# Scoring the paged keys of a decode step on TensorE, with one softmax over all eight requests

## The chip, the core and the metric

The kernel runs on one core of a Trainium2 chip. The metric is the device time of one execution in microseconds, from runs on the chip. Engines are named as in the profile: PE (matrix multiplies; PEld is its weight load), DVE (vector), ACT (scalar, activations), POOL (GpSimd) and SP (it issues nearly all transfers here). One engine executes its instructions in the order in which the program holds them; a waiting instruction holds up all that stand behind it on that engine.

## What is computed

One layer of a decoder, on a prompt of 512 tokens and on eight sample requests of one token each. A mixer runs two kinds of heads beside each other (a gated recurrence and differential attention), then cross-attention to a memory, then a SwiGLU feed-forward layer. The change concerns the differential attention of the sample requests: each has 4096 past keys and values in 32 pages of 128 positions, found through a page table.

```python
def diff_weights(s, lam):
    p = jax.nn.softmax(s.astype(F32), axis=-1)
    return p[:, :, 0] - lam * p[:, :, 1]          # two maps of 64 dims per head

def diff_attn_sample(q, k, v, lam, k_past, v_past):
    scale = q.shape[-1] ** -0.5
    s_past = jnp.einsum('bqhmd,bkhmd->bhmqk', q, k_past).astype(F32) * scale
    s_new = jnp.einsum('bqhmd,bkhmd->bhmqk', q, k).astype(F32) * scale
    w = diff_weights(jnp.concatenate([s_past, s_new], axis=-1), lam).astype(v.dtype)
    return (jnp.einsum('bhqk,bkhv->bqhv', w[..., :P], v_past)
            + jnp.einsum('bhqk,bkhv->bqhv', w[..., P:], v))
# past keys and values of a request: cache[page_table[b]], 32 pages of (128, 4 heads, 128)
```

## The kernel before

Everything is fp32. The large products of the prompt are made of two rounded parts of each operand (a `hi` part, rounded by ACT, and the remainder `lo`, made by DVE) and three matmuls per tile; these are the `mm` matmuls, 3072 of them. Their weights stream through a ring of three `raw` buffers, 512 KB a transfer, in the order of `plan`: w_in (28 transfers), w_mk and w_mv (16), w_out, w_mq and w_mo (24), then w_gate, w_up and w_down. I use the first transfer of w_mk, of w_out and of w_gate as marks that cut the program in four stages.

The order of instructions on each engine is set when the program is built. Generators (`load_keys`, `sum_values`, the heads, ...) are streams that a scheduler, `Weave`, resumes one at a time, by rank and by the times of a built-in estimate, `Clock`. What it chooses becomes the fixed order of each engine, SP among them: a page transfer that waits for its buffer holds up the weights behind it.

The sample's attention before: `load_keys` spills the query, broadcasts one request's query to all partitions (`qb`), and gathers two pages (2 x 256 KB) into one of `KBUFS` = 3 buffers, request after request. `weigh_keys` multiplies a buffer by `qb` in place, on POOL in pieces of 256 columns or on DVE; `sum_keys` reduces it on DVE to scores (`sc`). When a request's 16 pairs are done, `sample_softmax` makes its softmax, and `load_values` and `sum_values` gather four pages of values at a time and multiply them on PE (`pv`), four matmuls beside each other in 32 columns of the array each. So values of request 0 are read while keys of request 1 are. `value_out` adds a request's result to `oda_s`.

Behind the attention stands `sample_rest`: it waits for `done["values"]` and for `S["da"]`, and runs the sample's output projection, cross-attention (`cmk`, `cqb`, `cmv`) and the norm that gives `S["h2"]`. The sample's feed-forward layer needs `S["h2"]`: weights that pass in the prompt's ring after it is there are used in passing (`follow`), those that passed before are read a second time (`s_ffn_alone`, tiles `gu`, `g`, `dn`).

## Time and profile before

| | |
|---|---|
| runs | 1158.51, 1160.65, 1164.11 us; median 1160.65 us |
| profiled execution | 1162.99 us, its span 1161.2 us |
| busy share of the span | PE 91%, DVE 70%, POOL 46%, ACT 38% |
| mean granted PE clock | 0.956 of full |
| transfers | 293.68 MB, 253 GB/s in the mean |

The span runs from the first to the last instruction; the profiled execution takes 1.8 us more than its span. A busy PE has a matmul in flight, which is not the same as a PE at its peak rate. The busy shares are means over stages that differ, so the sections below go by stages.

### The profile page before, as it was taken

To read this page: it belongs to the slowest core of one execution; us is meant where nothing else is said; L and a number is where in the kernel's file an instruction comes from. 1 tells how busy PE (TensorE), PEld (TensorE's weight loads), DVE (VectorE), ACT (ScalarE), POOL (GpSimd) and SP (SyncE) were. 2 spreads that over 40 slices of the span, in tenths; PEclk is the share of its full clock that TensorE was granted. 3 is DMA by queue.
4 is the path that set the end of the run, shared out by engine and by line. 5 is a ranking of instruction groups with operands and counts; after the bars stand their busy time and mean duration, and the time that the engine had idled before them with its cause. 6 is when DMAs were issued, how large, how long until landed. Compare 5 with 4: busy or idle time off the path is not lost.

```text
span 1161.2 us, 21190 instructions
## 1 busy us (share of the span) xinstructions
PE 1052.9 (91%) x6624; PEld 722.7 (62%) x6624; DVE 813.4 (70%) x1318; ACT 444.2 (38%) x980; POOL 534.0 (46%) x590
## 2 busy tenths in 40 slices
PE   7999977886878899999889899999998789999997
PEld 5666756664444566566546667667666557666666
DVE  6698979999989857778667857758535864334135
ACT  5423434456455643335323322313223433132123
POOL 0259677479644736464857648567002420000001
PEclk9999897897889899999979999999999899999999
DMA  7656544664897899898878797898995897489792
GB/s 263 224 153 215 191 147 134 152 190 153 271 279 253 306 330 313 290 325 283 274 236 292 261 306 243 290 311 264 331 364 137 258 319 242 157 307 355 268 350 82
DMA packets 172563, 293.68 MB, mean 253 GB/s; under 512 B 17185, under 2 KB 38050, under 8 KB 172450
## 3 DMA queue, kind: packets, MB, share of 16 engines
q1 hardware_dynamic: 171218, 291.22, 76.3%
q8 instruction: 52, 0.85, 0.3%
q10 hardware_dynamic: 1232, 1.11, 0.3%
q14 instruction: 61, 0.50, 0.1%
HBM read 283.18 MB, written 9.08 MB: 252 GB/s over the span
## 4 chain that ended last, share of the span: by engine, by line
PE 53%; DVE 18%; DMA 15%; POOL 5%; issue 4%; SPq 2%; ACT 1%; DVEq 0%; POOLq 0%; ACTq 0%
PE mm L305 37%; PE pv L305 6%; DMA cache_k<-cache_k 4%; DVE lx L305 3%; POOL cache_k L305 3%; DMA cache_v<-cache_v 3%; DVE sc L305 3%; DVE lo L305 3%; DMA cqb<-cqd 2%; PE sgu L305 2%; DMA kv<-vd 2%; SPq L305 2%; PE sdn L305 1%; DMA raw<-w_down 1%; PE sgm L305 1%
## 5 line engine op out<-in xcount | busy, mean ns | idle before, releaser
L305 POOL TENSOR_TENSOR cache_k<-cache_k,qb 128x256 f32<-128x256 f32 x500 | 440.1, 915 | 238.4 <-DMA cache_k<-cache_k 213.4
L305 PE MATMUL mm<-sh,hi 128*128 128x512 f32 (+1 forms) x832 | 343.0, 412 | 1.5 <-ACT hi L305 1.5
L305 PE MATMUL mm<-sh,lo 128*128 128x512 f32 (+1 forms) x832 | 324.9, 390 | 15.6 <-DVE lo L305 15.3
L305 DVE TENSOR_TENSOR lo<-raw,hi 128x512 fp32r<-128x512 f32 (+1 forms) x260 | 204.9, 792 | 187.7 <-ACT hi L305 157.3
L305 ACT CAST hi<-raw 128x512 fp32r<-128x512 f32 (+1 forms) x260 | 157.3, 606 | 445.1 <-PE mm L305 411.8
L305 PE MATMUL mm<-sl,hi 128*128 128x512 f32 (+1 forms) x832 | 324.1, 390 | 0.0
L305 PEld LDWEIGHTS mm<-sh,hi 128*128 128x128 f32 x832 | 157.6, 189 | 91.2 <-issue 52.7
L305 PEld LDWEIGHTS mm<-sh,lo 128*128 128x128 f32 x832 | 157.7, 190 | 53.9 <-DVE lo L305 20.3
L305 DVE TENSOR_REDUCE sc<-cache_k 128x16 f32<-128x1024 f32 x128 | 154.9, 1212 | 48.7 <-POOL cache_k L305 48.6
L305 PEld LDWEIGHTS mm<-sl,hi 128*128 128x128 f32 x832 | 158.0, 190 | 27.1 <-issue 0.7
L305 PE MATMUL pv<-cache_v,sc 128*32 128x512 f32 x512 | 90.7, 644 | 6.3 <-DMA cache_v<-cache_v 5.5
L305 POOL TENSOR_TENSOR res<-res,par 128x512 f32<-128x512 f32 x2 | 2.1, 1042 | 187.5 <-ACT rsq L305 187.1
L305 PE MATMUL mm<-hi,sh 128*128 128x512 f32 x128 | 56.0, 437 | 0.2 <-DVE zg L305 0.2
L305 DVE TENSOR_TENSOR res<-mm,res 128x512 f32<-128x512 f32 (+1 forms) x68 | 43.0, 653 | 16.5 <-PE mm L305 16.4
L305 POOL TENSOR_TENSOR cache_k<-cache_k,cqb 128x512 f32<-128x512 f32 x8 | 13.1, 1642 | 88.9 <-DMA cqb<-cqd 85.6
L305 PE MATMUL mm<-lo,sh 128*128 128x512 f32 x128 | 52.6, 411 | 0.2 <-DVE lo L305 0.2
L305 PE MATMUL mm<-hi,sl 128*128 128x512 f32 x128 | 52.3, 408 | 0.0
L305 PEld LDWEIGHTS pv<-cache_v,sc 128*32 128x32 f32 x512 | 15.3, 111 | 41.7 <-DMA cache_v<-cache_v 19.8
L305 PE MATMUL mm<-hi,mh 128*128 128x512 f32 x64 | 31.2, 487 | 0.4 <-DVE ohg L305 0.4
L305 PEld LDWEIGHTS mm<-hi,sh 128*128 128x128 f32 x128 | 25.4, 198 | 7.9 <-issue 2.3
L305 PEld LDWEIGHTS mm<-hi,sl 128*128 128x128 f32 x128 | 25.4, 198 | 5.8
L305 PEld LDWEIGHTS mm<-lo,sh 128*128 128x128 f32 x128 | 25.3, 198 | 5.4 <-DVE lo L305 0.6
(411 smaller groups left out, 1392.9 us busy)
## 6 DMA issues: line engine op xcount, KB each, us to landing
cache_k<-cache_k SPq DMA_DIRECT2D x256, 256.0 KB, 4.3
cache_v<-cache_v SPq DMA_DIRECT2D x256, 256.0 KB, 4.3
raw<-w_in SPq DMA_DIRECT2D x27, 512.0 KB, 4.8
raw<-w_down SPq DMA_DIRECT2D x22, 512.0 KB, 6.4
raw<-w_gate SPq DMA_DIRECT2D x20, 512.0 KB, 5.6
raw<-w_up SPq DMA_DIRECT2D x20, 512.0 KB, 5.5
dn<-w_down SPq DMA_DIRECT2D x36, 256.0 KB, 6.2
cmv<-cache_mem_v SPq DMA_DIRECT2D x32, 256.0 KB, 5.0
```

What stands on the lines that cost most here:

```text
L305: ins = getattr(self.engine, op)(*a, **k)
```

## The change

The host lays the pages of `cache_k` out with the key's 128 dimensions as rows and (head, position) as columns. `place_queries` puts the eight rotated queries into two zeroed tiles (`qst`) so that for each request and head a 128 x 32 block holds the two maps' halves in the two columns of that request. `score_keys` takes the gathered page pairs of two requests at a time and multiplies them on PE: 16 matmuls of 32 x 128 for each two buffers, four beside each other, which accumulate the scores of all eight requests in a shared bank (`ks`). Four such banks are copied to `wt`. `load_keys` now goes over the page pairs first and over the eight requests inside; there are four key buffers, released two by two. `weigh_keys`, `sum_keys` and the `qb` broadcasts go. There is one softmax, after the last key; ACT's exponential sums its rows, and 16 matmuls (`wt`) turn the weights into the layout that `sum_values` needs. Values are asked for only when the keys are nearly done, and used only after the softmax.

```diff
-SLOTS = 66
+SLOTS = 67
-KBUFS = 3
+KBUFS = 4
-KRANK = 1
+KRANK = 2
...
     def load_keys():
-        qd = spill(S["q"], "qd")
         for n in range(NB * nst):
-            b, s = divmod(n, nst)
-            if s == 0:
-                yield lambda: b - SC_BUFS < done["out"]
-                yield clock.next("row", 3)
-                qb = row("qb")
-                load_row(qb, qd, b)
-                scs_of[b] = ring(sp, [P, NPG, 8], "sc", SC_BUFS, "sc")
+            s, b = divmod(n, NB)
             yield lambda: n - KBUFS < done["keys"]
             yield clock.next("cache_k", KBUFS)
             kt = ring(kp, [P, KPG, T], "cache_k", KBUFS, "cache_k")
             gather("cache_k", b, KPG * s, [kt[:, i, :] for i in range(KPG)])
-            raw_keys.append((n, kt, qb))
-
-    def weigh_keys():
...
             kts[n] = kt
 
-    def sum_keys():
...
+    def score_keys():
+
+        yield lambda: "qst" in S
+        for n in range(0, NB * nst, 2):
+            s, b0 = divmod(n, NB)
+            if b0 == 0 and s % 4 == 0:
+                yield from pv_room()
+                acc = pvt("ks")
+            yield lambda: n + 1 in kts
+            yield (kts[n], kts[n + 1], *qst)
+            cols = slice(s % 4 * P, (s % 4 + 1) * P)
+            for y in range(2):
+                for b in (b0, b0 + 1):
+                    for g in range(4):
+                        h = 2 * (g % 2) + y
+                        mm(
+                            acc[32 * g : 32 * g + 32, cols],
+                            qst[b // 4][:, b % 4, h, :],
+                            kts[n + b - b0][:, g // 2, h * P : (h + 1) * P],
+                            b + y == 0,
+                            b + y == NB,
+                        )
+            done["keys"] = n + 2
+            if b0 == NB - 2 and s % 4 == 3:
+                yield (acc,)
+                yield from room()
+                w = wts[s // 4] = slot("wt")
+                dve.tensor_reduce(mx4[:, s // 4 : s // 4 + 1], acc, axis=AX.X, op=ALU.max)
+                act.copy(w, acc)
+                pv_give()
+        give(2)
+        weave.add(sample_softmax(), KRANK)
...
     def load_values():
         for n in range(NB * NCH):
-            yield lambda: n - VBUFS < done["values"] and done["keys"] > (n // NCH + 1) * nst - KEYS_LEFT
+            yield lambda: n - VBUFS < done["values"] and done["keys"] > NB * nst - KEYS_LEFT
...
     def sum_values():
         for n in range(NB * NCH):
             b, s = divmod(n, NCH)
-            yield lambda: n in vts and done["soft"] > b
+            yield lambda: n in vts and done["soft"] == NB
...
-        weave.add(weigh_keys(), PRANK)
-        weave.add(sum_keys(), KRANK, "d")
-        weave.add(sample_softmax(), 2, "d")
+        weave.add(place_queries(), 2)
+        weave.add(score_keys(), KRANK)
...
-        "cache_k": i["cache_k"].reshape(n_phys, PG * 512),
+        "cache_k": np.ascontiguousarray(i["cache_k"][0].transpose(0, 3, 2, 1)).reshape(n_phys, PG * 512),
```

On SP, in the middle of the w_in weights, before the change: one gather of two pages (the table read, register work, two `cache_k` transfers) and the next weights (`raw`), then a query broadcast in place of weights once per request.

```order
L305 DMA raw214_1493<-w_in 128x2x512
L919 TENSOR_LOAD ptab_81
L919 ISA x4
L305 ISA
L305 DMA cache_k226_1568<-cache_k 128x512
L305 ISA
L305 DMA cache_k226_1568<-cache_k 128x512
L305 DMA qb227_1590<-qd_494 128x4x128
L305 DMA raw231_1611<-w_in 128x2x512
```

After the change, the same engine and the same part of w_in.

```order
L296 DMA raw207_1919<-w_in 128x2x512
L903 TENSOR_LOAD ptab_81
L903 ISA x4
L296 ISA
L296 DMA cache_k208_1921<-cache_k 128x512
L296 ISA
L296 DMA cache_k208_1921<-cache_k 128x512
L903 TENSOR_LOAD ptab_81
L903 ISA x4
L296 ISA
L296 DMA cache_k209_1946<-cache_k 128x512
```

Two more gathers of this form follow before the next `raw`. Ahead of the first weights of w_mk stand 204 page transfers of keys in place of 64; ahead of the first of w_out all 256, in place of 106 keys and 36 values; between the first of w_out and the first of w_gate 172 values, in place of 80 keys and 124 values; behind the first of w_gate 84 values, in place of 70 keys and 96 values.

On PE, early in w_in, before the change: the matmuls of one weight tile follow each other.

```order
L305 MATMUL mm113_653<-sh22_153,hi100_585 128x512
L305 MATMUL mm113_653<-sl23_154,hi100_585 128x512
L305 MATMUL mm113_653<-sh22_153,lo101_595 128x512
L305 MATMUL mm121_671<-sh22_153,hi100_585 128x512
L305 MATMUL mm121_671<-sl23_154,hi100_585 128x512
```

After the change, the 16 score matmuls of two gathered buffers (`cache_k121`, `cache_k126`) stand among the matmuls of one weight tile.

```order
L296 MATMUL mm129_780<-sh22_154,hi93_495 128x512
L296 MATMUL mm129_780<-sl23_155,hi93_495 128x512
L296 MATMUL mm129_780<-sh22_154,lo101_598 128x512
L296 MATMUL ks104_647<-cache_k121_720,qst99_586 32x128 x4
L296 MATMUL ks104_647<-cache_k126_754,qst99_586 32x128 x4
L296 MATMUL ks104_647<-cache_k121_720,qst99_586 32x128 x4
L296 MATMUL ks104_647<-cache_k126_754,qst99_586 32x128 x4
L296 MATMUL mm132_831<-sh22_154,hi93_495 128x512
```

There are 64 such clusters, 1024 score matmuls; the hardware records an fp32 matmul as two, so the trace would show 2048. The weights that the sample's feed-forward layer reads a second time fall from 30.4 MB to 18.9 MB, and all transfers of the program's SP from 291.2 MB to 277.3 MB.

## Rows read from the trace of the kernel before

**Rows 1.** Busy time by stage: us, each engine (instructions), PE clock, DMA share, GB/s.

```profile
core 0: us, PE busy (x) PEld busy (x) DVE busy (x) ACT busy (x) POOL busy (x), PEclk, DMA share, GB/s
0.00:237.00 237.00, 204.02 (x1943) 153.22 (x1944) 201.09 (x326) 102.02 (x224) 129.32 (x146) 0.94 0.61 185
237.00:389.00 152.00, 120.99 (x683) 76.81 (x682) 136.26 (x260) 82.23 (x213) 101.56 (x112) 0.88 0.74 237
389.00:626.00 237.00, 225.39 (x1112) 145.88 (x1111) 174.43 (x260) 99.62 (x211) 143.94 (x164) 0.96 0.88 294
626.00:1161.00 535.00, 502.49 (x2892) 346.83 (x2890) 301.57 (x475) 160.35 (x333) 159.22 (x170) 0.99 0.80 270
```

**Rows 2.** The chain that ended last, by line, of each stage in turn.

```profile
by line: DVE lx L305 15.8%; PE mm L305 11.7%; issue 8.6%; DVE lo L305 8.5%; DVE sc L305 8.1%; DMA raw<-w_in 4.5%; DMA cache_k<-cache_k 3.7%; POOL cache_k L305 3.4%; POOL aT L305 2.1%; DMA xt<-xpT 2.0%; DVE rt L305 2.0%; DVE bhg L305 2.0%; S
by line: DMA kv<-vd 14.9%; DMA cache_v<-cache_v 10.7%; PE mm L305 7.1%; issue 7.0%; DVE sc L305 6.2%; DVE lo L305 5.2%; DVE st L305 4.3%; POOL cache_k L305 4.2%; PE oda L305 3.4%; DVE ml L305 3.3%; DVE rt L305 3.2%; DVE ro L305 2.4%; DVE pm
by line: PE mm L305 44.9%; PE pv L305 14.3%; DMA cache_v<-cache_v 7.5%; DMA cache_k<-cache_k 6.3%; PE co L305 5.4%; issue 3.3%; PE cs L305 2.5%; SPq L305 1.9%; SPq L919 1.8%; PE sgm L305 1.7%; PE ss L305 1.6%; PE oda L305 1.5%; DVE sc L305 
by line: PE mm L305 53.0%; PE pv L305 5.3%; DMA cqb<-cqd 5.2%; DMA cache_k<-cache_k 4.7%; PE sgu L305 4.3%; POOL cache_k L305 4.1%; PE sdn L305 2.6%; DMA raw<-w_down 2.6%; PE sgm L305 1.7%; DMA cmk<-cache_mem_k 1.7%; PE cpv L305 1.7%; SPq L
```

**Rows 3.** Costliest groups of the page: the removed work, and the idle time before it.

```profile
L305 POOL TENSOR_TENSOR cache_k<-cache_k,qb 128x256 f32<-128x256 f32 x500 | 440.1, 915 | 238.4 <-DMA cache_k<-cache_k 213.4
L305 DVE TENSOR_REDUCE sc<-cache_k 128x16 f32<-128x1024 f32 x128 | 154.9, 1212 | 48.7 <-POOL cache_k L305 48.6
```

**Rows 4.** DVE's key reductions and remainders, stage one; then the reductions of stage two.

```profile
L305 DVE TENSOR_TENSOR lo<-raw,hi 128x512 fp32r<-128x512 f32 x52 | 41.9, 809 | 12.8 <-ACT hi L305 8.1 <-DMA 256079_356<-w_in 4.4
L305 DVE TENSOR_REDUCE sc<-cache_k 128x16 f32<-128x1024 f32 x30 | 36.2, 1210 | 9.9 <-POOL cache_k L305 9.9
...
L305 DVE TENSOR_REDUCE sc<-cache_k 128x16 f32<-128x1024 f32 x22 | 26.6, 1211 | 4.1 <-POOL cache_k L305 4.1
```

**Rows 5.** SP's transfers in order of time: start us, us, xcount.

```profile
19.27 1.54 SPq L305 DMA_DIRECT2D raw<-w_in  x2
...
236.69 0.39 SPq L305 DMA_DIRECT2D raw<-w_mk  x1
...
388.76 0.39 SPq L305 DMA_DIRECT2D raw<-w_out  x1
...
436.34 0.86 SPq L305 DMA_DIRECT2D cache_k<-cache_k  x2
437.30 0.39 SPq L305 DMA_DIRECT2D raw<-w_out  x1
439.00 0.86 SPq L305 DMA_DIRECT2D cache_k<-cache_k  x2
...
448.61 1.90 SPq L305 DMA_DIRECT2D cache_v<-cache_v  x4
...
481.38 5.58 SPq L305 DMA_DIRECT2D cache_v<-cache_v  x8
...
625.78 0.39 SPq L305 DMA_DIRECT2D raw<-w_gate  x1
```

**Rows 6.** Transfers at their densest, three stretches of 50 us; columns as in rows 1.

```profile
400.00:450.00 50.00, 50.00 (x254) 31.48 (x250) 33.66 (x47) 23.12 (x45) 27.95 (x31) 1.00 0.93 314
800.00:850.00 50.00, 47.61 (x232) 32.80 (x231) 27.69 (x46) 14.06 (x23) 10.48 (x13) 1.00 0.95 319
```

**Rows 7.** Pieces of the whole chain: start us, us, records in the piece.

```profile
706.57 11.12 PE mm L305 x48
...
744.76 1.85 PE pv L305 x16
...
1011.51 3.59 PE sgm L305 x64
```

**Rows 8.** PE's narrow fp32 matmuls of 32 weights by 128 columns: busy us, mean ns.

```profile
L305 PE MATMUL sacc<-raw,hs 128*32 128x128 f32 x320 | 12.5, 278 | 7.3 <-DMA raw<-w_in 6.1 <-DVE hs L305 1.2
```

**Rows 9.** The `mm` tiles alone, by stage: PE busy (records) first.

```profile
0.00:237.00 237.00, 159.15 (x605) 114.75 (x606) 7.86 (x12) 8.20 (x12) 0.94 0.61 185
...
389.00:626.00 237.00, 139.33 (x557) 101.51 (x558) 13.38 (x20) 1.37 (x2) 0.96 0.88 294
626.00:1161.00 535.00, 411.24 (x1695) 305.92 (x1693) 64.17 (x100) 0.00 (x0) 0.99 0.80 270
```

**Rows 10.** DMA issues: engine, count, KB each, median us from issue to landing.

```profile
cache_k<-cache_k SPq DMA_DIRECT2D x256, 256.0 KB, 4.3
```

**Rows 11.** What SP's queue waited for in stage one: us in total, times, longest.

```profile
SPq L305 <- DVE lo L305: 34.7, 15, 9.2
SPq L305 <- DVE sc L305: 27.4, 13, 6.8
SPq L305 <- DVE st L305: 10.7, 2, 7.2
```

More of the change, by code (lines that the diff above doesn't have):

```diff
@@ L461, in row @@
     def row(s):
-        return ring(sp, [P, T], "row", 3, s)
+        return ring(sp, [P, T], "row", 2, s)
     def mm(out, a, b, start, stop):
@@ L497, in decode_step @@
     ident, ropes, cmask = views["ident"], views["ropes"], views["cmask"]
[L498 removed]
+    rep32 = views["rep32"]
     pvsel = views["pvsel"].rearrange("p (h n) -> p h n", h=HEADS)
@@ L965, in sum_keys @@
-    def sum_keys():
-        for n in range(NB * nst):
-            b, s = divmod(n, nst)
-            yield lambda: n in kts
-            yield (kts[n],)
-            dve.tensor_reduce(
-                scs_of[b][:, KPG * s : KPG * (s + 1), :].rearrange("p n c -> p (n c)"),
-                kts[n].rearrange("p n (c d) -> p (n c) d", d=64),
-                axis=AX.X,
-                op=ALU.add,
-            )
-            done["keys"] = n + 1
-    def sample_softmax():
-        for b in range(NB):
-            yield lambda: "sn" in S and "lam" in S and done["keys"] >= (b + 1) * nst
-            sc = scs_of[b]
-            mx = ksmall([P, 8], "mx")
-            dve.tensor_reduce(mx, sc.rearrange("p n c -> p c n"), axis=AX.X, op=ALU.max)
-            yield
+            kts[n] = kt
@@ new lines, in sample_softmax @@
+    def sample_softmax():
+        yield lambda: "sn" in S and "lam" in S
+        mx = ksmall([P, 1], "mx")
+        dve.tensor_reduce(mx, mx4, axis=AX.X, op=ALU.max)
+        yield
+        yield from at_room()
+        pt = att("mxt")
+        tr(pt[:1, :P], mx, ident)
+        yield (pt,)
+        dve.tensor_tensor(m_new, pt[:1, :64], s_new, op=ALU.max)
+        w2 = wide.rearrange("p (g c) -> p g c", g=2)
+        dve.tensor_tensor(m_new, m_new, pt[:1, 64:P], op=ALU.max)
+        at_give()
+        dve.tensor_scalar(w2, m_new.unsqueeze(1).to_broadcast([1, 2, 64]), -1.0, None, op0=ALU.mult)
+        dve.tensor_tensor(p_new, s_new, m_new, op=ALU.subtract)
+        yield
+        yield from at_room()
+        pb = att("mxb")
+        mm(pb[:, :1], wide, ones[:1, :1], True, True)
+        yield (pb,)
+        nm = ksmall([P, 1], "nm")
+        dve.tensor_copy(nm, pb[:, :1])
+        at_give()
+        z4 = ksmall([P, 4], "z4")
+        yield
+        for i, w in enumerate(wts):
+            act.activation(w, w, AF.Exp, bias=nm, accum_out=z4[:, i : i + 1])
+        act.activation(p_new, p_new, AF.Exp)
+        yield
+        z1 = ksmall([P, 1], "z1")
+        dve.tensor_reduce(z1, z4, axis=AX.X, op=ALU.add)
+        yield
+        yield from at_room()
+        pz = att("zt")
+        for i in range(2):
+            mm(pz[:1, :64], z1, ident[:, 64 * i : 64 * i + 64], i == 0, i == 1)
+        yield (pz,)
+        dve.tensor_tensor(r_new, pz[:1, :64], p_new, op=ALU.add)
+        at_give()
+        dve.reciprocal(r_new, r_new)
+        r3 = r_new.rearrange("p (c m) -> p c m", m=2)
+        dve.tensor_tensor(r3, r3, lamc[:1].unsqueeze(1).to_broadcast([1, 32, 2]), op=ALU.mult)
+        dve.tensor_copy(w2, r_new.unsqueeze(1).to_broadcast([1, 2, 64]))
+        yield
+        yield from at_room()
+        pr_ = att("cf")
+        mm(pr_[:, :1], wide, ones[:1, :1], True, True)
+        yield (pr_,)
+        rw = ksmall([P, 1], "rw")
+        dve.tensor_copy(rw, pr_[:, :1])
+        at_give()
+        turn = quadt("turn", tag="fq", bufs=3)
+        dve.tensor_scalar(
+            turn.rearrange("p (b g x) -> p b g x", b=NB, g=4),
+            ident.rearrange("p (g b x) -> p b g x", b=NB, g=4), rw, None, op0=ALU.mult,
+        )
+        yield
+        for i, w in enumerate(wts):
@@ L985, in sample_softmax @@
             yield from at_room()
-            pt = att("mxt")
-            tr(pt[:8, :P], mx, ident)
+            pt = att("wt")
+            p5 = pt.rearrange("p (j b k c) -> p j k b c", j=2, b=NB, k=2)
+            for c in range(4):
+                mm(p5[:, c // 2, c % 2], w[:, c * P : (c + 1) * P], turn, True, True)
             yield (pt,)
-            m1 = ksmall([8, 1], "m1")
-            dve.tensor_reduce(m1, pt[:8, :P], axis=AX.X, op=ALU.max)
+            act.copy(w, pt)
             at_give()
-            dve.tensor_tensor(mT[:, b : b + 1], m1, snT[:, b : b + 1], op=ALU.max)
@@ L1059, in value_out @@
     def value_out(b, pvs):
-        yield lambda: ("cf", b) in S and done["out"] == b
-        wsel = quadt("wsel", (P, 4, 32), "wsel", 2)
-        dve.tensor_scalar(wsel, pvsel[:, :, 7 - b : 39 - b], cfs[:, b : b + 1], None, op0=ALU.mult)
-        yield
+        yield lambda: done["out"] == b
+        yield (pvs,)
         yield from at_room()
@@ L1075, in value_out @@
         if b == NB - 1:
+            give(4)
             S["da"] = True
```

135 lines of the change are left out of this document (43 added, 92 removed).

## Prediction, before the changed kernel was run

> **What bounds the kernel now.** I read the windows by stage first, cut at the first weights of w_mk, w_out and w_gate [rows 1, 5], then the chain of each stage [rows 2], then single groups. The page alone misleads: PE is busy 91% of the span, but the 3072 `mm` matmuls at their densest take 11.12/48 = 0.232 us each [rows 7], 712 us in all, so PE often has something in flight and does not advance.
>
> The reader is to see four different limits. Stage A (0 to 237 us): DVE is busy 201 of 237 us, transfers run at 185 GB/s with the DMA engines 61% busy [rows 1]; the chain is DVE (`lx`, `lo`, key sums `sc`) [rows 2]. Stage B (237 to 389): DVE 136 of 152 us, and the chain names the value pages and the broadcast `kv` as DMA waits [rows 1, 2]. Stages C (389 to 626) and D (626 to 1161): DVE has room, PE `mm` is 45% and 53% of the chain, and the key path appears as waits: in C `cache_k` transfers 6.3%, in D 4.7% plus POOL's products 4.1% [rows 2]. POOL's 440 us are not a limit as such: it idled 213 us for keys [rows 3].
>
> **What goes.** POOL's 500 products (440 us), DVE's 128 sums of 1.212 us (155 us) [rows 3], 2.1 MB of query broadcasts and seven of eight softmaxes. In A that frees DVE of about 36 us, in B of 27 [rows 4]. A second relief is smaller: the mean `lo` is 0.809 us in A [rows 4]; how much of it is POOL's doing this view does not tell, and I count nothing for it.
>
> **What comes, on PE.** 2048 records of 32 weights by 128 columns, four beside each other, so 512 groups. Low bound: 64 records of 256 columns took 3.59 us [rows 7], 0.224 us a group of four, half of it for 128 columns: 0.112, in all 57 us. High bound: the nearest row of equal shape, 320 records in 12.5 us [rows 8], 0.156 a group, 80 us; it includes the end of each short burst, and `ks` comes in bursts of eight groups. I take 60. The softmax's 16 `wt` matmuls and its chain of small steps replace eight such chains: counted as nothing, between a gain of some us and a loss of some us. The score banks' four copies and maxima are about 1 us of ACT and DVE each: nothing beside the 155 us.
>
> **What moves: the pages on SP.** The gathers themselves stay, 128 of keys and 64 of values; their place changes. Now count SP's issue time, since its program is one queue. From one key gather to the next with one weight transfer between is 439.00 - 436.34 = 2.66 us, of which the weights are about 0.5 (start of `raw` to its end and a gap): 2.16 a gather of two pages. Two gathers of four values took 5.58 us from the first transfer to the end of the eighth; with 1.90 for one gather's own four transfers, 3.68 per gather [rows 5]. Full DMA engines move 314/0.93 to 319/0.95, 336 GB/s [rows 6].
>
> Stage A after (transfers and bytes are counted in the order of SP's instructions): 204 page transfers in place of 64. From the fifth weight transfer at 19 us [rows 5] on (nothing changes ahead of it) SP has 102 gathers x 2.16 = 220, and 67 other transfers x 0.5 = 34: 254 us, so A cannot end before 273. By bytes alone, 76 MB/336 = 226 us, 245 with the start. PE needs 605 x 0.232 = 140 [rows 9], 0.8 x 60 = 48 for the scores and the heads' small matmuls beside: it fits. DVE falls from 201 to 165: it fits too. So SP's own issue time becomes the limit of A. Waits of SP for late remainders, recurrent states and buffers were 73 us in three rows [rows 11]; `sc` goes, and a queue that is itself late meets most others ready. I add 12: **A = 285, 48 later than before**.
>
> The Trainium skill (DMA: Bandwidth & Descriptors, section "Issuing engines are not separate DMA queues") says that the time a sequencer takes to initiate a DMA is usually small relative to the DMA. By that rule A would go by the bytes, 245 us, 28 less than by the queue; here two pages take SP 2.16 us and 0.524 MB/336 = 1.56 us of DMA, so the row does not bear it out.
>
> Stage B after: 52 key transfers, no values; SP 26 x 2.16 + 50 x 0.5 = 81 and 31 MB/336 = 92 us, both below DVE's 136 - 27 = 109. The waits for value pages on the chain (10.7%, 16 us [rows 2]) go, those for `kv` stay. I take off DVE's 27 us less 2 for the one softmax: **B = 127, 25 less**.
>
> Stage C after: 172 values, no keys. SP 43 x 3.68 + 34 x 0.5 = 175; 60.3 MB/336 = 179. PE before: 557 x 0.232 = 129 [rows 9], and on the chain `pv` 34, `co`, `cs`, `sgm`, `ss`, `oda` together 30 [rows 2]: 193. With 172 for 124 value transfers `pv` is 47: 206. So 44 us of the 237 were waits; the 15 for keys go, value waits (18) stay, and some replace: **C = 226, 11 less**.
>
> Stage D after: PE 1695 x 0.232 = 393 [rows 9] and `pv`, `sgu`, `sdn`, `sgm`, `cpv` 15.6% of 535, 83 us [rows 2]: 476, three less for 84 values in place of 96. (`pv`: 16 records in 1.85 us [rows 7].) Over it stood 59. The key path on the chain was 8.8%, 47 us [rows 2]; 11.5 MB of second weight reads, 34 us of DMA, go since `S["h2"]` comes earlier. The `cqb` waits (28 us) only move. I give back 40: **D = 495**.
>
> Sum 285 + 127 + 226 + 495 = 1133 us, 28 below the span of 1161.2. The profiled execution (1162.99) lies 1.8 over its span and 2.3 over the median of 1160.65, so against the median this is 1133 again: **1133 us**, 2.4% faster.
>
> **Rivals.** (1) *Slower: the key ring starves SP in A.* Two buffers are freed at a time, so SP can run only two gathers ahead (4.3 us and weights: 254/51 = 5.0 us a round). A landing takes 4.3 us [rows 10], one cluster's eight groups 0.9 to 1.2: 5.2 to 5.5, just under the 5.0 and the 1 us or so of register work ahead of SP's next wait. If landings under dense traffic take 5.5 to 6, SP waits 1 us in each of 51 rounds and PE stands with it: A = 336, total 1184. For: traffic in A rises from 185 to near 300 GB/s. Against: PE's slack. It decides from 0.55 us of wait a round, where all other gains are eaten. (2) *Much faster:* A by the bytes (257 with the same 12), and C and D down to PE's need: 257 + 127 + 206 + 473 = 1063; half of that way is 1098. It needs SP to hide its register work; the 2.66 us speak against. (3) *The same:* the key waits of C and D were only what the chain happened to name, and PE's own pace or the value transfers take their place; half of the 51 us comes: 1159. That the change doesn't do what it says I exclude: POOL's and DVE's instructions are gone from the program.
>
> **How the numbers follow.** Forecast 0.48; rival (1) 0.24, between 1160 and 1190; (2) 0.15, near 1085; (3) 0.13. Within 0.5% is what a measurement here can't tell from no change (1155 to 1166). Faster: the forecast's, (2)'s and little else, 0.62; same 0.14; slower 0.24. The forecast's own range is 1110 to 1155: PE's price of the scores (57 to 80) is covered in A unless SP is quicker, waits in A 0 to 30, C and D 30 to 70. To hold eight in ten: 1085 to 1180.
>
> **What would show it.** Right: SP's first w_mk weights near 285 us, later than 237, with gathers 2.16 us apart and DMA share in A up to 0.8; DVE's busy time down by about 150; `ks` about 60 us of PE; w_out near 412; `cache_k` gone from the chain behind it; `sdn` starting well before 1000 us. Wrong: SP waiting for PE's `ks` in A by over 28 us, PE stalls on `ks` with landings over 5.5 us, or stage D near 535.

## The result and the profile after

| | before | after |
|---|---|---|
| median | 1161.34 us (1158.51 to 1164.11) | 1210.61 us (1208.17 to 1212.12) |
| profiled execution | 1162.99 us | 1210.4 us, its span 1208.6 |

The ratio is 1.042 (1.039 to 1.045): the changed kernel is 4.2% slower. The forecast was 1133 us, its range ended at 1180.

From the page of the changed kernel, the busy times and the costliest groups of the scores (out<-in, count | busy, mean ns | idle time just before them, and what ended it); POOL was at 46% and DVE at 70%:

```profile
PE 1120.7 (93%) x8721; PEld 766.9 (63%) x8721; DVE 567.6 (47%) x1118; ACT 443.8 (37%) x978; POOL 93.2 (8%) x92
...
L296 PE MATMUL ks<-cache_k,qst 128*32 128x128 f32 x2048 | 89.0, 286 | 26.2 <-DMA cache_k<-cache_k 25.4
L296 PEld LDWEIGHTS ks<-cache_k,qst 128*32 128x32 f32 x2048 | 57.7, 112 | 60.9 <-DMA cache_k<-cache_k 37.8
```

The windows of its four stages, cut at the same transfers as in [rows 1]:

```profile
core 0: us, PE busy (x) PEld busy (x) DVE busy (x) ACT busy (x) POOL busy (x), PEclk, DMA share, GB/s
0.00:303.00 303.00, 270.22 (x3680) 195.34 (x3681) 147.76 (x316) 109.40 (x236) 33.35 (x45) 0.97 0.84 267
303.00:464.00 161.00, 128.83 (x999) 89.44 (x998) 93.90 (x248) 93.78 (x244) 16.31 (x13) 0.92 0.68 200
464.00:676.00 212.00, 211.93 (x1122) 131.85 (x1122) 92.69 (x162) 84.50 (x176) 10.84 (x9) 1.00 0.84 282
676.00:1208.00 532.00, 509.73 (x2926) 350.30 (x2925) 233.28 (x394) 156.08 (x324) 32.72 (x25) 0.98 0.62 202
```

DVE has room in every stage now, so what was to be taken from it was taken. A and B became longer, and there no engine is busy throughout: 33 us of A and 32 of B have no matmul in flight (33 and 31 before, [rows 1]; PE's busy time in A grew by 66 us; `ks` is busy 67 there). In C and D PE is busy 212 of 212 and 510 of 532 us. The chain by line of A, of B and of D (the rows that answer to [rows 2]):

```profile
by line: PE mm L296 20.2%; DMA cache_k<-cache_k 19.1%; SPq L296 9.8%; PE ks L296 8.8%; DMA raw<-w_in 8.6%; SPq L903 6.9%; issue 6.5%; PE sacc L296 2.1%; DMA vd<-svq 1.5%; DMA xt<-xpT 1.5%; ACT sr L296 1.2%; DVE zf L296 1.1%; PE ohg L296 1.0
...
by line: DMA kv<-vd 25.6%; DMA cache_k<-cache_k 16.2%; SPq L296 9.2%; issue 6.2%; PE ks L296 5.3%; PE mm L296 4.9%; ACT pr L296 4.7%; SPq L903 4.5%; DVE pmx L296 2.6%; ACT kv L296 2.4%; PE sc L296 2.4%; ACT hi L296 2.1%; DVE lo L296 1.7%; P
...
by line: PE mm L296 67.6%; PE sgu L296 4.7%; PE pv L296 4.6%; DMA cqb<-cqd 3.4%; PE sdn L296 3.2%; DMA raw<-w_up 1.8%; PE cpv L296 1.8%; PE sgm L296 1.7%; DVE lo L296 1.6%; DVE sg L296 1.3%; DMA raw<-w_gate 1.1%; DMA cache_v<-cache_v 1.0%; 
```

In A, DVE is gone from the front of the list and key landings and SP's own time (`SPq`, 16.7%, 51 us) stand in its place. In B the landings of `kv`, the value rows of the sample's recurrence, are a quarter of the chain, 41 us. What SP waited for in A (us, times, longest):

```profile
SPq L296 <- PE sacc L296: 8.6, 2, 8.4
SPq L296 <- DVE lo L296: 4.9, 4, 2.4
SPq L296 <- DMA vd<-svq: 3.5, 1, 3.5
SPq L296 <- PE mm L296: 3.4, 4, 2.7
SPq L296 <- PE ks L296: 3.4, 11, 0.4
```

Rival (1), SP starved by the key ring, would show in the last of these rows: 3.4 us. It did not happen.

One relief is larger than was forecast. DVE's busy time fell from 813 to 568 us, by 246, and the sums were 155 of it. The remainders `lo` are the same 260 instructions in the kernel before, in the changed one (183.1 us, 705 ns each) and in e6_no_key_work below, which is the kernel before without POOL's products and with DVE's sums cut to two columns in 64 (the kernel before first):

```profile
L305 DVE TENSOR_TENSOR lo<-raw,hi 128x512 fp32r<-128x512 f32 (+1 forms) x260 | 204.9, 792 | 187.7 <-ACT hi L305 157.3
```

```profile
L308 DVE TENSOR_TENSOR lo<-raw,hi 128x512 fp32r<-128x512 f32 (+1 forms) x260 | 182.7, 705 | 343.8 <-ACT hi L308 294.2
```

So this was what the forecast called the second relief and counted as nothing: without the removed work the same DVE instruction takes 705 ns instead of 792.

All kernels of the study, with the lengths of their four stages in the profiled execution (cut at the first weights of w_mk, w_out and w_gate), for the sections below. Ratios are to runs of the kernel before made beside each (medians from 1160.5 to 1165.6 us); differences in us below are between the medians of this table:

| kernel | median us | ratio to before (95%) | A | B | C | D |
|---|---|---|---|---|---|---|
| before | 1161 | | 237 | 152 | 237 | 535 |
| after | 1210.6 | 1.042 (1.039 to 1.045) | 303 | 161 | 212 | 533 |
| e1_double_scores | 1224.8 | 1.055 (1.051 to 1.059) | 318 | 162 | 215 | 528 |
| e2_half_scores | 1206.6 | 1.040 (1.036 to 1.043) | 299 | 157 | 215 | 531 |
| e3_fixed_pages | 1179.7 | 1.015 (1.011 to 1.019) | 279 | 156 | 214 | 530 |
| e4_paced_keys | 1212.3 | 1.043 (1.038 to 1.047) | 264 | 154 | 225 | 569 |
| e5_kv_ahead | 1209.5 | 1.038 (1.032 to 1.044) | 306 | 157 | 204 | 540 |
| e6_no_key_work | 1110.2 | 0.954 (0.948 to 0.960) | 210 | 140 | 234 | 523 |
| e7_pe_scores_old_order | 1192.6 | 1.025 (1.020 to 1.030) | 315 | 165 | 227 | 483 |
| e8_kv_plain | 1177.6 | 1.010 (1.005 to 1.016) | 301 | 129 | 214 | 532 |
| e9_old_order_paced | 1185.8 | 1.020 (1.014 to 1.027) | 244 | 150 | 226 | 564 |
| e10_kv_on_pe | 1190.6 | 1.024 (1.018 to 1.029) | 305 | 148 | 215 | 522 |
| e11_before_rows_on_pe | 1161.9 | 1.001 (0.999 to 1.003) | 240 | 135 | 243 | 543 |
| e12_fixed_and_plain | 1151.4 | 0.991 (0.988 to 0.994) | 271 | 134 | 216 | 529 |
| e13_paced_half | 1176.7 | 1.013 (1.007 to 1.019) | 245 | 150 | 221 | 562 |
| e14_no_bounds_check | 1153.4 | 0.994 (0.991 to 0.997) | 278 | 143 | 208 | 521 |
| e15_pairs_of_gathers | 1165.4 | 1.004 (1.002 to 1.007) | 292 | 128 | 214 | 530 |
| e16_before_no_check | 1141.5 | 0.981 (0.977 to 0.985) | 237 | 151 | 224 | 528 |
| e17_after_no_check | 1175.8 | 1.011 (1.008 to 1.013) | 285 | 156 | 210 | 526 |
| e18_paced_later_scores | 1236.5 | 1.063 (1.060 to 1.066) | 257 | 144 | 242 | 593 |

### The profile page after: what moved, and what is told of

Same layout as the page of the kernel before. It is cut to its first block, busy times and chain, and to the rows that moved or that the text cites. A ratio compares the mean times of both kernels' runs of the same rounds, so it can differ in the third digit from the quotient of the medians.

```text
span 1208.6 us, 24350 instructions
## 1 busy us (share of the span) xinstructions
PE 1120.7 (93%) x8721; PEld 766.9 (63%) x8721; DVE 567.6 (47%) x1118; ACT 443.8 (37%) x978; POOL 93.2 (8%) x92
## 4 chain that ended last, share of the span: by engine, by line
PE 66%; DMA 16%; SPq 6%; DVE 5%; ACT 3%; issue 3%; DVEq 0%; ACTq 0%
PE mm L296 46%; DMA cache_k<-cache_k 7%; PE pv L296 6%; SPq L296 4%; DMA kv<-vd 3%; PE ks L296 3%; SPq L903 2%; DMA raw<-w_in 2%; PE sgu L296 2%; DMA cqb<-cqd 2%; PE sdn L296 1%; DVE lo L296 1%; PE sgm L296 1%; PE co L296 1%; DMA raw<-w_up 1%
## 5 line engine op out<-in xcount | busy, mean ns | idle before, releaser
L296 DVE TENSOR_TENSOR lo<-raw,hi 128x512 fp32r<-128x512 f32 (+1 forms) x260 | 183.1, 705 | 468.2 <-ACT hi L296 413.5
L296 PEld LDWEIGHTS mm<-sh,lo 128*128 128x128 f32 x832 | 157.9, 190 | 50.9 <-DVE lo L296 16.7
L296 PE MATMUL ks<-cache_k,qst 128*32 128x128 f32 x2048 | 89.0, 286 | 26.2 <-DMA cache_k<-cache_k 25.4
L296 PEld LDWEIGHTS ks<-cache_k,qst 128*32 128x32 f32 x2048 | 57.7, 112 | 60.9 <-DMA cache_k<-cache_k 37.8
L296 PE MATMUL pv<-cache_v,wt 128*32 128x512 f32 x512 | 79.9, 604 | 0.5 <-DMA cache_v<-cache_v 0.5
L296 PEld LDWEIGHTS pv<-cache_v,wt 128*32 128x32 f32 x512 | 13.5, 108 | 32.0 <-issue 21.5
L296 POOL TENSOR_TENSOR res<-sh,sl 128x512 f32<-128x512 f32 x8 | 10.6, 1346 | 258.8 <-DMA cache_v<-cache_v 253.8
```

The costliest lines, as they stand in the source:

```text
L296: ins = getattr(self.engine, op)(*a, **k)
```

## The experiments

### What the score matmuls cost where they stand

The first theory, Q, puts the loss on SP's queue: 204 page transfers stand ahead of the weights of w_mk, and PE has slack beside them. Theory P says that PE's own need sets the whole span, so that the scores are added in full. Every score matmul twice:

```diff
-                            b + y == NB,
+                            False,
                         )
+                        real.tensor.matmul(  # the same operands
+                            start=False, stop=b + y == NB)
```

> Changed kernel with every score matmul issued twice (the scores double, so the output is not the reference's); order and transfers unchanged. Theory Q (SP's queue: the loss is made where 204 key transfers stand ahead of the first w_mk weights, PE has slack there): 57 us of added PE work is mostly covered, 1210 to 1225. Theory P (PE's own need sets the whole span, so the score matmuls add their time in full): 1210 + 57, about 1265.

1224.8 us, 14 more. And half of them (heads 1 and 3) left out:

```diff
-                        mm(acc[...], qst[...], kts[...], b + y == 0, b + y == NB)
...
+                        if y: clock.count("pe", "matmul", [out], [wq, kx])
+                        else: mm(out, wq, kx, b == 0, b == NB - 1)
```

> Changed kernel without the score matmuls of heads 1 and 3 (512 of 1024 left out, output not the reference's); order and transfers unchanged. Q: 1205 to 1210. P: 1210 - 28, about 1182.

1206.6 us, 4 less. The group of the page in the two runs, doubled (the second copies have a row of their own, 118.3 us, which overlaps this one) and halved:

```profile
L296 PE MATMUL ks<-cache_k,qst 128*32 128x128 f32 x2048 | 120.1, 283 | 7.7 <-DMA cache_k<-cache_k 6.8
```

```profile
L299 PE MATMUL ks<-cache_k,qst 128*32 128x128 f32 x1024 | 62.5, 290 | 33.5 <-DMA cache_k<-cache_k 30.6
```

PE's idle time ahead of `ks`, nearly all of it for key landings, goes 33.5, 26.2, 7.7 as the matmuls go 1024, 2048, 4096: where PE waits for pages, more matmuls mostly fill the wait. In this place, with SP's queue as it is, their number is not what costs. P falls for A and B; without any scores the changed kernel was not run.

### SP's work for the pages

Key pages at fixed addresses, without table reads and register work on SP (the pages are not those of the table):

```diff
+        if which == "cache_k":
+            for i, t in enumerate(dst):
+                sync.dma_start(t, ckv[which][(7 * (c + i)) % n_phys])
+            return
```

> Changed kernel with key pages at fixed addresses: the same transfers in the same order, but no table read and register work ahead of them, so SP issues a key transfer in about 0.45 us in place of 1.06 (output not the reference's). Q: stage A goes from 303 us to the bytes' pace, 250 to 265, and the total to 1165 to 1180. P: the span stays within 10 us of 1210.

1179.7 us, 31 less, 23 of it in A. Q holds for the whole, at the weak end; A at 279 stayed longer than its 250 to 265. What SP waited for in A of this run shows the next limit:

```profile
SPq L296 <- PE ks L296: 71.7, 40, 5.0
```

With its register work gone SP stands 72 us for key buffers that the scores have not yet freed (3.4 in the changed kernel), which is what rival (1) described, and PE is busy 261 of the 279 us. Next, the same keys spread out in time; the scheduler makes the order anew:

```diff
-            yield lambda: n - KBUFS < done["keys"]
+            yield lambda: n - KBUFS < done["keys"] and n <= 2.33 * (len(raws) - 5)
```

> Changed kernel with the key gathers paced along the weights (gather n not before weight transfer 5 + n/2.33), so that the keys end near the 60th weight transfer and not the 44th. Q: about 56 gathers in place of 102 stand ahead of w_mk, stage A falls from 303 to about 235, and the total to 1150 to 1175. P: within 10 us of 1210, since PE's work is the same.

1212.3 us: P's number, and Q missed. A fell by 39 us (Q had 68) and B by 7, and all of it came back, 13 in C and 36 in D. The windows of C and D in this run:

```profile
418.00:642.00 224.00, 213.18 (x1541) 149.68 (x1542) 95.49 (x175) 87.45 (x184) 11.03 (x9) 0.99 0.78 250
642.00:1210.00 568.00, 543.45 (x3103) 352.28 (x3101) 234.59 (x398) 159.86 (x329) 32.77 (x25) 0.99 0.76 248
```

PE is busy 543 us in D, 33 more than in the changed kernel. The scores that left A and B stand in C (27 us of PE), and values of C moved to D: 188 transfers in place of 84, with `pv` busy 66 us there instead of 31. They land on a PE that is full. In this run a page costs in front by SP's queue and behind by PE, and spreading the keys gained nothing.

### What the removal is worth by itself

The kernel before, POOL's products and DVE's sums left out, every other instruction in its place (no scores are computed; DVE still reduces two columns in 64):

```diff
-            dve.tensor_reduce(out, keys, axis=AX.X, op=ALU.add)
+            clock.count("dve", "tensor_reduce", [out], [keys])
+            real.vector.tensor_reduce(out, keys[:, :, :2], axis=AX.X, op=ALU.add)
...
-                        pool.tensor_tensor(kt[:, i, cols], kt[:, i, cols], qb[:, cols], op=ALU.mult)
+                        clock.count("pool", "tensor_tensor", [kt[:, i, cols]], [kt[:, i, cols], qb[:, cols]])
```

> The kernel before with POOL's products and DVE's sums left out (DVE reduces two columns of each group of 64 in their place, so scores are not computed); the order of every other instruction is unchanged. It shows what the removal alone is worth. Theory R (the removal frees what the forecast took: about 36 + 27 us in A and B and 50 in C and D, less what other limits keep): 1075 to 1110. Theory F (from about 450 us on PE is full anyway, and in front the removed work was hidden in good part): 1125 to 1150. Rival (3) of the forecast, that the key waits were only what the chain named: 1150 to 1161.

1110.2 us, 54 less by the ratio (47 to 61); theory R, at its upper end. The windows of its stages, beside [rows 1]:

```profile
0.00:210.00 210.00, 193.25 (x1934) 146.81 (x1935) 137.82 (x326) 98.43 (x219) 24.43 (x35) 0.98 0.67 209
210.00:350.00 140.00, 116.81 (x690) 75.02 (x689) 93.93 (x258) 84.33 (x218) 26.34 (x22) 0.91 0.81 255
350.00:584.00 234.00, 223.84 (x1109) 145.06 (x1110) 117.25 (x261) 99.43 (x211) 12.68 (x9) 0.98 0.89 297
584.00:1108.00 524.00, 500.45 (x2895) 347.80 (x2893) 246.44 (x470) 159.92 (x333) 30.41 (x25) 0.98 0.82 276
```

A gives 27 us, B 12, C 3 and D 12. In D, PE is busy 500 us with the key work gone and was busy 502 with it [rows 1]: nearly all the waits of D that the chain had put down to keys stood beside matmuls in flight.

### The broadcasts of `kv` in stage B

Asked for one request earlier (`fetch(b + 1)` ahead of the work on b):

```diff
+            (st, kv), ahead = ahead, fetch(b + 1) if b + 1 < NB else None
-            st = slot("st")
-            sync.dma_start(st, io["state"][b])
-            kv = slot("kv")
-            load_row(kv, vd, b)
```

> The changed kernel, in which the recurrence's stream asks for the state and the value row `kv` of the next request before it works on the present one (two more slots held meanwhile; everything computed). Stage B took 161 us where 127 were forecast, and its chain names landings of `kv` for 41 us. Theory V (these landings set B's length): ACT's waits for `kv` fall from 39 us to under 10, B to 130 to 145, the whole to 1180 to 1198. Rival S (the landings only end last; SP, which comes late to everything while 52 key transfers stand in its queue, sets B): ACT's waits fall, B stays within 8 of 161 and the whole within 6 of 1210.

1209.5 us: nothing. ACT's waits for `kv`, 38.9 us before, are gone altogether, and B's chain names key landings in their place (28.2%). The order is a little different (16 value transfers now stand in B), so the plainest sign is when the last scores were made, below: no earlier than before. The wait alone was not the cost. Read plainly instead of broadcast (another tensor's data, so the sample's recurrence is not the reference's):

```diff
-            load_row(kv, vd, b)
+            sync.dma_start(kv, io["state"][b])
```

> The changed kernel with the broadcast of one value row to all partitions (`kv`, 128 x 512) replaced by a plain read of 256 KB of the same shape (another tensor's data, so the sample's recurrence is not the reference's). Theory V (the landings of `kv`, 8.5 to 12.6 us, set stage B): landings of 4 to 6 us, B 135 to 150, the whole 1185 to 1200. Rival S: landings shorter or not, the whole within 6 of 1210.

1177.6 us, 33 less; B is 129, 32 shorter. The landings in the changed kernel and windows of it while broadcasts were under way (issued at 302.1, 367.8, 393.7 and 412.1 us):

```profile
DMA to landing us min/median/max: 8.5/9.2/12.6
```

```profile
306.13:310.13 4.00, 4.00 (x46) 3.02 (x45) 3.72 (x8) 3.94 (x9) 1.34 (x2) 1.00 0.89 34
...
371.00:375.00 4.00, 3.71 (x37) 2.81 (x37) 2.61 (x10) 1.11 (x5) 0.00 (x0) 1.00 0.36 79
...
398.00:402.00 4.00, 2.36 (x33) 1.44 (x27) 3.79 (x13) 1.42 (x5) 0.00 (x0) 1.00 0.27 67
...
416.00:420.50 4.50, 4.41 (x32) 3.96 (x32) 4.15 (x14) 1.61 (x3) 0.00 (x0) 1.00 0.26 49
```

With the plain read:

```profile
DMA to landing us min/median/max: 5.0/5.5/5.6
```

Of each of the eight broadcasts, the 4 us that begin 4 us after its issue move only 34 to 88 GB/s, while pages are wanted. The busy share of the DMA engines in them differs, 0.22 to 0.91, so how a broadcast holds them up these rows don't tell; its 256 KB go in 512 packets of 512 bytes, those of the plain read in 128 of 2 KB. On B's chain the page at 335.9 us, issued behind the broadcast of 333.6, took 13.1 us to land (the median of all is 4.1), and PE ran dry behind it:

```profile
344.00:348.00 4.00, 0.00 (x0) 0.00 (x0) 0.00 (x0) 1.70 (x6) 0.00 (x0) 0.69 0.89 268
348.00:352.00 4.00, 3.63 (x28) 2.33 (x29) 3.88 (x6) 1.14 (x3) 1.59 (x1) 0.50 1.04 371
```

It has no matmul in flight from 344 to 348 us, and the clock granted from 348 on is 0.50 (the lower level, 1.2 GHz). The same rows made on PE, everything computed:

```diff
-            load_row(kv, vd, b)
+            pk = att("kvb")
+            for h in range(HEADS):
+                r = 32 * h + b
+                mm(pk[:, h * P : (h + 1) * P], ident[:, r : r + 1].to_broadcast([P, P]), svq, True, True)
...
```

> The changed kernel with the eight broadcasts of value rows (`kv`) made on PE, by four 128 x 128 matmuls with one column of the identity as repeated weights, in place of transfers; everything computed. The plain read in their place gave 33 us, asking for them earlier 1 us. Theory T (a broadcast of one row holds the DMA engines for some 5 us longer than its bytes, and the pages and weights behind it wait): 1172 to 1190, stage B 130 to 145. Rival U (the plain read gained because it did not wait for the value rows to be written out first): PE's broadcast waits for the same rows, so 1200 to 1212.

1190.6 us, 20 less: just above T's range, with B at 148. The order is anew here too: 20 value transfers now stand in B and 20 fewer in D, which is 11 us shorter. The first and last start of the score matmuls in the changed kernel, with `kv` asked for earlier, read plainly, and made on PE:

```profile
L296 PE MATMUL ks<-cache_k,qst x2048: 269/273/423, 44.5 to 398.5; 128*32 128x128 f32 x187
```

```profile
L296 PE MATMUL ks<-cache_k,qst x2048: 269/273/423, 44.3 to 402.9; 128*32 128x128 f32 x187
```

```profile
L296 PE MATMUL ks<-cache_k,qst x2048: 272/273/418, 45.5 to 373.9; 128*32 128x128 f32 x187
```

```profile
L296 PE MATMUL ks<-cache_k,qst x2048: 272/273/423, 44.6 to 370.2; 128*32 128x128 f32 x187
```

The keys are done 28 us sooner with the broadcasts on PE and 25 with the plain read, so rival U is out, and it is the broadcast transfers that hold the pages up. The same in the kernel before, there for the eight query rows (`qb`) too:

> The kernel before with its eight query broadcasts and eight value-row broadcasts made on PE in the same way, everything computed. Theory T: the same occupancy was paid in the kernel before, but there the first stage goes by DVE, with room on the DMA engines, so only the eight of `kv` and the later queries give something back: 1125 to 1150. Rival: hidden under DVE throughout, 1155 to 1166.

1161.9 us, ratio 1.001 (0.999 to 1.003): the rival's number, but not its reason, since B is 17 us shorter, and A, C and D give it back (3, 6 and 8). The order has changed: none of the 36 value transfers that stood in B does now, and D has 132 in place of 96. So this run doesn't tell what the broadcasts cost in the kernel before.

### Do the two costs in front add?

Fixed pages and plain `kv` together (the edits of e3_fixed_pages and e8_kv_plain):

> The changed kernel with both earlier edits at once: key page addresses fixed (no table read or register work on SP for keys) and `kv` read plainly (so neither output of the sample's mixer is the reference's). Apart they gave 31 and 33 us. Theory Q2 (two separate costs of the first 460 us, SP's register work and the broadcasts' hold on the DMA engines; behind both PE): they add, 1140 to 1152. Rival L (both shorten the same waits of PE for pages, and PE's own work stands next): 1162 to 1180.

1151.4 us: 59 of the 64 that they gave apart. They are two costs, and together more than the 49 us by which the change lost. The window of A in this run:

```profile
0.00:271.00 271.00, 256.01 (x3676) 190.94 (x3676) 146.77 (x315) 108.05 (x234) 33.15 (x45) 0.99 0.89 299
```

Against the run without key work (e6_no_key_work) A is still 61 us longer, B 6 and C 18 us shorter and D 6 longer. In this A PE is busy 256 of 271 us (193 of 210 there) and the DMA engines are 89% busy (67% there): with both costs out, the scores' work and the pages' bytes stand close behind, and no run parts these two.

### The order of before with the scores on PE

```diff
-        weave.add(weigh_keys(), PRANK)
-        weave.add(sum_keys(), KRANK, "d")
+        weave.add(score_keys(), KRANK)   # a bank per request, 8 matmuls per gather
...
+                    mm(acc[32 * g : 32 * g + 32, cols], ident[:, :32], kts[n][:, g // 2, h * P : (h + 1) * P], y == 0, y == 1)
```

> The kernel before with the scores on PE, in the order of before: keys request after request, one softmax a request, values of a request behind its keys (the weights of these matmuls are rows of the identity, so the output is not the reference's; the matmuls have the number and shape of the changed kernel's). The built-in scheduler makes its order anew. Theory Q (the loss comes from the 204 key transfers ahead of w_mk and from nothing of PE): 1120 to 1150, faster than before. Theory P (PE's score matmuls are the price): the run without key work plus 50 to 80 us, 1175 or more. If it is within 15 us of 1210 the order has no part in the loss.

1192.6 us: Q is missed, and P's number is met (82 over the run without key work). It does not tell the two apart all the same: released from DVE, the scheduler had put 150 keys and 76 values ahead of w_mk, and A is 315. So with the old places enforced (a table of 128 numbers, weights ahead of each gather):

```diff
-            yield lambda: n - KBUFS < done["keys"]
+            yield lambda: n - KBUFS < done["keys"] and len(raws) >= KEY_AT[n]
```

> As the run with the scores on PE in the old order (keys request after request, a softmax a request, identity rows as weights, so the output is not the reference's), but gather n of keys is not asked for before as many weight transfers as stood ahead of it in the kernel before. In the unpaced run the scheduler had put 150 key and 76 value transfers ahead of the first weights of w_mk and 220 + 124 ahead of w_out; here 60 + 12 and 102 + 64 (kernel before: 64 + 0 and 106 + 36). Theory Q (the loss is made by page transfers ahead of the weights in SP's queue; the scores cost PE little): the run without key work (1110) plus 5 to 35 us: 1115 to 1145, the first w_mk weights at 200 to 225 us. Theory P (with PE full behind 400 us, the scores' 89 us of busy PE count nearly in full): 1165 to 1190.

1185.8 us, 76 over the run without key work, which has its pages in nearly the same places. Q fails here; P's number is met. Half of these matmuls left out:

> The paced run in the old order (scores on PE, 1186 us) with half of the score matmuls left out and every other instruction where it was. In the changed kernel the same edit gave only 4 us. Theory P2 (where the scores stand beside a PE that is full, they count with nearly all their time: 89 to 97 us busy for 2048): 1135 to 1155. Rival W (what costs there is PE standing at its queue's head until a page has landed, which half the matmuls do as well): 1170 to 1186.

1176.7 us: 9 less, so rival W's number, and not P's. Then the scores two gathers later, with five buffers in place of three (`SLOTS` 62 for 66):

```diff
-            yield lambda: n in kts
+            yield lambda: min(n + 2, NB * nst - 1) in kts
```

> The paced run in the old order (1186 us) with two more key buffers (four slots fewer elsewhere) and the scores of a page pair placed only after the transfers of the pair after next have been issued, so that PE meets landed pages. Theory W (what the scores cost there is PE standing at the head of its queue for a landing; half the matmuls had given 9 us): PE's idle time ahead of `ks` falls from 70 us to under 25 and the whole to 1135 to 1160. Rival P (PE's own work and the four slots): 1175 to 1195.

1236.5 us: both theories missed. The idle time ahead of `ks` that ended with a key landing fell from 70.2 to 26.7 us on PE and its weight load together, nearly as W has it, but up to the first w_gate weights the run is 23 us later than the paced one (643 against 620), and its last 94 us hold the sample's feed-forward layer by itself, with the weights of `gu` and `dn` read a second time. What the 76 us are in the old order stays open: not the number of matmuls alone (9 for half), not the waits ahead of them alone.

### Less work on SP in a full version

The `ISA x4` behind each table read, in SP's rows shown with the change, check the two page numbers against the size of the cache. The table's numbers are valid, so the check can be left out:

```diff
             ptab[:, c : c + len(dst)], [mybir.EngineType.SP], min_val=0, max_val=n_phys - 1
+            , skip_runtime_bounds_check_because="the page table holds pages of the cache"
```

With `kv` on PE beside it:

> The changed kernel with `kv` on PE (1191 us) and without the four bounds-check instructions that stand on SP behind each table read (the pages are gathered through the table as before; everything computed). Theory Q: the four are a good part of the 2.1 us that SP takes for two pages; 1160 to 1178, gathers below 1.7 us. Rival L: SP is quicker, but PE's wait for landings and its own work stay: 1180 to 1190.

1153.4 us, 37 less than with the check, and just below the kernel before: 0.994 (0.991 to 0.997). SP's timeline in the changed kernel and in this run, four gathers between weights (start, length, transfers):

```profile
105.09 7.34 SPq L296 DMA_DIRECT2D cache_k<-cache_k  x8
113.69 0.39 SPq L296 DMA_DIRECT2D raw<-w_in  x1
115.37 7.71 SPq L296 DMA_DIRECT2D cache_k<-cache_k  x8
123.19 0.39 SPq L296 DMA_DIRECT2D raw<-w_in  x1
```

```profile
98.83 5.73 SPq L296 DMA_DIRECT2D cache_k<-cache_k  x8
106.69 0.39 SPq L296 DMA_DIRECT2D raw<-w_in  x1
107.86 6.48 SPq L296 DMA_DIRECT2D cache_k<-cache_k  x8
```

and the scores' group on its page:

```profile
L296 PE MATMUL ks<-cache_k,qst 128*32 128x128 f32 x2048 | 72.1, 276 | 4.5 <-DMA cache_k<-cache_k 3.6
```

From the first transfer to the end of the eighth there are three gathers and the issue of two transfers (0.86 where a gather stands alone): (7.34 - 0.86)/3 = 2.16 us a gather, and (5.73 - 0.86)/3 = 1.62 without the check (the first row of each; the longer ones hold waits as well). With pages coming sooner, the same 2048 matmuls wait 4.5 us instead of 26.2 and are busy 72 instead of 89. Two things are in this. The `ks` matmuls alone, in two stretches of the changed kernel and in one of this run:

```profile
50.00:100.00 50.00, 12.68 (x320) 8.57 (x320) 0.00 (x0) 0.00 (x0) 0.00 (x0) 1.00 0.85 264
...
303.00:350.00 47.00, 10.38 (x190) 6.18 (x192) 0.00 (x0) 0.00 (x0) 0.00 (x0) 0.84 0.80 202
```

```profile
50.00:100.00 50.00, 12.07 (x352) 9.07 (x352) 0.00 (x0) 0.00 (x0) 0.00 (x0) 1.00 0.89 292
```

At a granted clock of 1.00 (2.4 GHz) a record is busy 40 ns in the changed kernel and 34 here; where the clock was at its lower level for a part of the time, 0.84 in the mean, it is 55. One table read for the pages of two requests on top:

> As the run without bounds checks, with one table read for the four pages of two requests' gathers, two key buffers asked for together (everything computed). Theory Q: SP falls to about 1.2 us for two pages, pages then go by bytes; 1145 to 1170. Rival L: within 6 of the run without bounds checks.

1165.4 us: inside Q's range, but 12 us slower than the run that it was to better, so nothing was gained. Two gathers at a time put 236 page transfers ahead of w_mk (212 in the run before), and A is 14 us longer.

The changed kernel with the check left out and nothing else:

> The changed kernel without the bounds checks and with nothing else changed (`kv` by transfers; everything computed; order unchanged). With `kv` on PE the same edit gave 37 us. Theory Q: SP's register work costs in the first 460 us whatever `kv` does: 1170 to 1182. Rival (the two belong together, since the broadcasts hold the pages up anyway): 1190 to 1208.

1175.8 us, 35 less, as Q has it, 18 of it in A: SP's cost is there whatever `kv` does. And the control, the kernel before without the check:

> The kernel before without the bounds-check instructions behind its table reads; its order of instructions is otherwise unchanged and everything is computed. A control for the fast full version: is the gain of 37 us a matter of the new order, where SP's queue sets the first 460 us, or would the kernel before have had it too? Theory Q: in the kernel before DVE and then PE are the limits, so 1148 to 1162. Rival: the checks cost there as well, 1115 to 1140.

1141.5 us, 0.981 (0.977 to 0.985): 20 less, between the two numbers. A and B are as before (237, 151), so where DVE is the limit it costs nothing; C gives 13 and D 7. (In C the chain had named SP's own time, `SPq`, for 3.7%, 9 us [rows 2].) This is the fastest full version of the study. With the check out of both, the change still loses, 1175.8 against 1141.5.

## Why the prediction was wrong, step by step

**The removal** was worth something, but less than was taken: 25, 11 and 40 us in B, C and D (in A SP's queue was to eat DVE's 36). By itself it gave 27, 12, 3 and 12 in A to D, 54 us (e6_no_key_work).

**Stage A (285, was 303).** That SP is late, and what a gather costs it, were right: 2.16 us a gather was counted and is measured. The term that was too small is "I add 12" for SP's waits: from 19 us on its wait rows in A sum to 26.5 us, and 273 + 27 is 300. That SP's register work lengthens A is shown by three edits, which shorten it by 23, 18 and 27 us (e3_fixed_pages, e17_after_no_check, and e14_no_bounds_check against e10_kv_on_pe). More it does not give: taken out, SP waits for key buffers, and PE is busy 261 of 279 us. What the Trainium skill says of initiating a DMA (DMA: Bandwidth & Descriptors, section "Issuing engines are not separate DMA queues"), that it is usually small relative to the DMA, did not hold here: the gather's 2.16 us on SP stand against the forecast's 1.56 of DMA.

**Stage B (127, was 161)** is the first step that failed outright. "SP 26 x 2.16 + 50 x 0.5 = 81 and 31 MB/336 = 92 us, both below DVE's 136 - 27 = 109", and "those for `kv` stay". DVE did fall, to 94 us, and stopped being the limit. But the bytes did not move at 336 GB/s: B moved 200 in the mean, with some 4 us of 34 to 88 GB/s in each broadcast of `kv`, and the forecast had no term for that. [rows 2] named `kv` in B, and the forecast took it as a wait that stays as it was; e5_kv_ahead shows that without the wait the keys come no sooner, e8_kv_plain that without the broadcast B is 32 us less.

**Stage C (226, was 212)** came out better: PE's need of 206 was nearly all that was left.

**Stage D (495, was 533)** is the second step that failed, and the larger: "PE 1695 x 0.232 = 393 ... 476 ... Over it stood 59 ... I give back 40". PE's need was worked out at its densest rate. Its busy time in that stage was 502 of 535 us already [rows 1], so only 33 us had no matmul in flight, and e6_no_key_work, with the key path gone from DVE and POOL, gave back 12. The chain's 47 us of "key path" were for the most part places where a key came last beside work that went on anyway: PE is busy 500 us of D without the keys' work. Of those 12, some 3 were left in the changed kernel; what took the rest was not parted. "Stage D near 535" was one of the forecast's own signs of being wrong.

The four misses, 18 and 34 and 38 too little and 14 too much, are the 76 us between 1133 and the changed kernel's span.

**PE's price (60).** Busy 89 us, with 26 of idle time ahead of it, nearly all for key landings: 115. In front their number hid in waits (14 us for doubling, 4 for halving), so it is not what lost the time in A and B as long as SP is late there.

**The balance.** After minus before is 49. The removal gives 54, so the change brought 103 us of new cost. The register work and the broadcasts give back 59 of them (e12_fixed_and_plain), which is more than their share of what is new: both were also in the kernel before, where the checks alone cost 20 (e16_before_no_check), and what the broadcasts cost there is not known (e11_before_rows_on_pe changed the order). At least some 44 us stay. They stand in A, 61 us longer than without key work against 18 us less in B, C and D together, with PE and the DMA engines near full; how much is the scores and how much the pages' bytes was not parted, and e4_paced_keys shows only that the pages can't be moved for free. Of the rivals, (1) ended on the right side, by a mechanism that did not happen; (3) had the right reading of D.

## What to carry to other kernels

A stage freed of its limit goes to the next one, so work out each engine's and each queue's time for the new content of the stage, the sequencer's instructions per transfer included, and take an engine's need from its busy time there, not from its best rate elsewhere. A share of the chain is no price for its cause: in D of the kernel before it named 47 us for the keys, and 12 came; in C it named 9 us for SP's own time, and taking out the checks alone gave 13. Before moving many small gathers ahead of the weights, look at what the issuing queue does for each of them: taking four check instructions out of a gather gave 35 us in the changed kernel and 20 in the one before, where the whole change lost 49.

## What was not expected of the hardware

- Four bounds-check instructions behind a table read cost SP 2.16 - 1.62 = 0.54 us for each two pages, 35 us of the changed kernel's time and 20 of the kernel before.
- A broadcast of one 2 KB row to 128 partitions took 8.5 to 12.6 us to land where a plain 256 KB read took 5.0 to 5.6, and for some 4 us of it only 34 to 88 GB/s were moved. With it out of the way the keys were done 25 to 28 us sooner.
- The same 2048 matmuls are busy 72 or 89 us: 34 or 40 ns a record at a granted clock of 1.00, by how late their pages come, and 55 in a stretch at 0.84. The busy time of short bursts behind landings is no fixed price.
- A DVE instruction that was not changed (`lo`) takes 792 ns in the kernel before and 705 where POOL's 440 us of products and DVE's sums are gone.
